# Token stage of a two-layer decoder step: bias loads on GpSimd's queue, weights queued ahead of later tokens, five token buffers, and the second weight group five tiles behind with its weights split in four parts

## The chip, the cores and the metric

One Trainium2 chip, one core of it. The metric is the device time of one execution in microseconds; lower is better. TensorE (PE) multiplies, ScalarE (ACT) and VectorE (DVE) prepare its operands and take its results, GpSimd (POOL) and SyncE (SP) mostly issue transfers; ACT can issue transfers too, from the same queue that holds its arithmetic.

## The reference, cut to what matters

The program is one inference step of a two-layer decoder for a prompt of 1024 tokens with 16 meta tokens ahead of it and for 8 sample sequences of 8 tokens: 1104 rows of 1024 values. The change touches only the first projection of the first layer, and there the value columns of `w_in` (1024 columns from column 1024 on) and its 16 gate columns:

```
def rmsnorm(x, g):
    r = lax.rsqrt(jnp.mean(xf * xf, axis=-1, keepdims=True) + EPS)
    return xf * r * g
...
p = rmsnorm(x, norm_a) @ w_in
v  = p[..., 2 * HK:2 * HK + HV]
gi = p[..., 2 * HK + 2 * HV:2 * HK + 2 * HV + H_A]
gf = p[..., 2 * HK + 2 * HV + H_A:]
li = softcap(gi + b_ig)
lf = log_sigmoid(softcap(gf + b_fg))
```

Everything is float32. The kernel gets that precision by splitting each operand into a high and a low part and adding three products.

## The kernel before, in words

The token stage is the function `values_a`. Its rows lie in nine tiles: tile 0 holds the 64 sample rows and the 16 meta rows, tiles 1 to 8 hold 128 prompt rows each. The value columns are made in four groups `c` of 256. The text calls group 0 the first group and group 3 the second group, since they are the two that run while the tokens come in; the second group also carries the 16 gate columns, so its products have 272 columns. Groups 1 and 2 follow after the loop. The weights of one group are two pieces `z` of 512 KB (rows 0 to 511 and rows 512 to 1023).

The steps, with the names that the text uses:

- `load(i)` (line 718) brings token tile i from memory into a buffer `xin`; four buffers exist. SP issues it, and it waits until the buffer's last reader is done.
- `fetch(c, z)` (line 650) brings a weight piece into one of two buffers `wraw`.
- T(i), in the code `turn(i)` (line 726): eight TensorE transposes of tile i into four PSUM buffers `xps`, two for a tile.
- `halves(i)` (line 734): ACT casts the transposed tile to the high part `xh`, DVE subtracts to get the low part `xl`, two instructions each.
- `halve(c, z)` (line 655): four times ACT scales 128 weight rows by the norm's gain into `whi`, and DVE makes `wlo`. For the second group a last pair of instructions does the same for the gate columns of the whole piece, columns 256 to 272 of `whi` and `wlo`.
- `keep(i)` (line 740): DVE copies the transposed tile into one of three buffers `hs`, and POOL issues the store of it (`hD`), for a later reload.
- `squares(i)` (line 747): ACT squares tile i with a running sum and takes the root; DVE later takes the reciprocal (line 783), the row's norm factor.
- V(c, i), in the code `values(c, i)` (line 671): 24 products for group c and tile i, and `out`, the ACT copy (line 681) that scales the result by the norm factor.

In this stage the order on PE, SP, DVE and ACT is the order in which the code is written; each engine takes its instructions strictly in that order. POOL's order, and the place of other functions' instructions between them (the biases of `rec_prep`, the page table of `cache_loads`), comes from the scheduler. Iteration i of the loop at line 769 does V(0, i), then T(i + 2) and `halves(i + 2)`, then the reciprocal and the copy out of V(0, i), then loads, `keep(i + 2)`, `squares(i + 2)`, perhaps a piece of the second group's weights, and last V(3, i - LAG) with LAG = 3. Both pieces of the second group are split in iterations 1 and 2, one whole piece in each.

Of the kernel before, what the change touches and what calls it, by code (L numbers as in the profile page):

```python
# [8 lines left out]
F32 = mybir.dt.float32  # L9
F32R = mybir.dt.float32r  # L10
I32 = mybir.dt.int32
AF = mybir.ActivationFunctionType
# [5 lines left out]
P = 128  # L18
D = 1024
# [9 lines left out]
NT = len(TT)  # L29
# [22 lines left out]
class PairWeights:  # L52
# [15 lines left out]
    def load(self, x):  # L68
        c0 = x % 2 * DFF + x // 2 * 2 * P
        for i, r in enumerate(self.plain(x)):  # L70
            self.net.nc.sync.dma_start(r, self.w[:, c0 + i * P : c0 + i * P + P].rearrange("(k p) n -> p k n", p=P))
# [560 lines left out]
def values_a(self, v, kp, gates, w_in, c3):  # L632

    nc, I = self.nc, self.I
    E = mybir.EngineType
# [4 lines left out]
    W, raws, xin, xps, hr = {}, {}, {}, {}, {}  # L640

    with ExitStack() as cw, self.pool("ppA0", bufs=4, space=PSUM) as pp:
        self.wpools(cw, 2, 4)
        wr = self.wp
        xr = cw.enter_context(self.pool("xr", bufs=3, side="right"))
        rr, ss = (xr.tile([P, NT], F32, name=nm, bufs=1) for nm in ("rr", "ss"))
# [3 lines left out]
        def fetch(c, z, queue=nc.sync):  # L650
            c0 = 2 * HA * DK + 256 * c
            raw = raws[c, z] = wr.tile([P, 4, 256], F32, name=self.uid("wraw"), tag="wraw", bufs=2)
            queue.dma_start(raw, w_in[4 * z * P : 4 * z * P + 4 * P, c0 : c0 + 256].rearrange("(k p) n -> p k n", p=P))

        def halve(c, z):
            raw = raws.pop((c, z))
            n = 272 if c == 3 else 256
            hi, lo = W[c, z] = [wr.tile([P, 4 * n], F32R, name=self.uid(nm), tag=nm, bufs=4).rearrange(
                "p (k n) -> p k n", k=4) for nm in ("whi", "wlo")]
            if c == 2:  # L660
                self.split(raw, hi, lo)
                return
            for k in range(4):
                y = hi[:, k, :256]
                nc.scalar.activation(y, raw[:, k], AF.Copy, scale=G(4 * z + k))
                nc.vector.scalar_tensor_tensor(out=lo[:, k, :256], in0=raw[:, k], scalar=G(4 * z + k),
                                               in1=y.bitcast(F32), op0=ALU.mult, op1=ALU.subtract)
            if c == 3:
                self.split(gw[:, 4 * z : 4 * z + 4], hi[:, :, 256:], lo[:, :, 256:])

        def values(c, i):
            n, m = 272 if c == 3 else 256, size(i)
            ps = pp.tile([P, 512], F32, name=self.uid("tmps"), tag="mm0")
            for k in range(KT):
                h, l = self.x_tile(i, k)
                wh, wl = W[c, k // 4]
                self.mm3(ps[:m, :n], h, l, wh[:, k % 4], wl[:, k % 4], k == 0, k == KT - 1)

            def out():
                r = 1.0 if c == 2 else rr[:m, i : i + 1]  # L680
                nc.scalar.activation(v(i)[:m, 2 * c : 2 * c + 2, :DV],
                                     ps[:m, :256].rearrange("p (h d) -> p h d", h=2), AF.Copy, scale=r)
                if c == 3:
                    nc.scalar.activation(gates[:m, i, :], ps[:m, 256:272], AF.Copy, scale=r)
            return out

        def reload(i):
            n, (t0, t1) = size(i), TT[i]
            y = hr[i] = xr.tile([P, KT, P], F32, name=f"hr{i}", tag="hr")
            nc.sync.dma_start(y[:, :, :n], self.hD[:, :, t0:t1])  # L690
# [21 lines left out]
        lx = ExitStack()  # L712
        lp = lx.enter_context(self.pool("lx"))
        tp = lx.enter_context(self.pool("lxp", bufs=4, space=PSUM))
        junk = lp.tile([P, D], F32, name="xsq")
        cell = lambda nm: lp.tile([P, D], F32, name=nm, tag="xin", bufs=4)

        def load(i):
            x = xin[i] = cell(f"xin{i}")
            if i == 0:  # L720
                nc.sync.dma_start(x[:NS], I["x_sample"].rearrange("b t d -> (b t) d"))
                nc.sync.dma_start(x[NS:T0], I["meta_tokens"])
            else:
                nc.sync.dma_start(x, I["x_prompt"][0, (i - 1) * P : i * P, :])

        def turn(i):
            n = size(i)
            for g in range(2):
                ps = xps[i, g] = tp.tile([P, 4, P], F32, name=self.uid("xps"), tag="xps")
                for k in range(4):  # L730
                    f = 4 * g + k
                    nc.tensor.transpose(ps[:, k, :n], xin[i][:n, f * P : (f + 1) * P], self.ident[:n, :n])

        def halves(i):
            n, (t0, t1) = size(i), TT[i]
            for g in range(2):
                ks = slice(4 * g, 4 * g + 4)
                self.split(xps[i, g][:, :, :n], xh[:, ks, t0:t1], xl[:, ks, t0:t1])

        def keep(i):  # L740
            n, (t0, t1) = size(i), TT[i]
            hs = lp.tile([P, KT, P], F32, name="hs", bufs=3)
            for g in range(2):
                nc.vector.tensor_copy(hs[:, 4 * g : 4 * g + 4, :n], xps.pop((i, g))[:, :, :n])
            nc.gpsimd.dma_start(self.hD[:, :, t0:t1], hs[:, :, :n])

        def squares(i):
            n = size(i)
            nc.scalar.activation(junk[:n], xin.pop(i)[:n], AF.Square, accum_out=ss[:n, i : i + 1])
            nc.scalar.activation(rr[:n, i : i + 1], ss[:n, i : i + 1], AF.Sqrt, scale=1.0 / D, bias=self.eps[:n])  # L750

        LAG = 3
        for z in range(2):
            fetch(0, z, nc.scalar)
            load(z)
        load(2)
        load(3)
        gw = xr.tile([P, P], F32, name="gw", tag="rb").rearrange("p (k n) -> p k n", k=KT)
        nc.scalar.dma_start(gw, w_in[:, 3072:3088].rearrange("(k p) n -> p k n", p=P))
        turn(0)  # L760
# [5 lines left out]
        halves(1)  # L766
        squares(0)
        keep(1)
        for i in range(NT + LAG):
            if i < NT:  # L770
                out = values(0, i)
            if i == 0:
                nc.vector.tensor_tensor(out=gw, in0=gw, in1=self.gain[:, G_A : G_A + KT].unsqueeze(2).broadcast_to([P, KT, 16]),
                                        op=ALU.mult)
                rows = xr.tile([P, P], F32, name="growsF", tag="rb")[: NG - G_F]
                self.gains(rows)
            if i + 2 < NT:
                turn(i + 2)
                halves(i + 2)
            if i == 0:  # L780
                squares(1)
            if i < NT:
                nc.vector.reciprocal(rr[: size(i), i : i + 1], rr[: size(i), i : i + 1])
                out()
            if i < 2:
                fetch(3, i)
            if i + 4 < NT:
                load(i + 4)
            if i + 2 < NT:
                keep(i + 2)  # L790
                squares(i + 2)
            if 1 <= i < 3:
                halve(3, i - 1)
            if i == 5:
                ps = tp.tile([P, 4, P], F32, name="gpsF", tag="xps").rearrange("p a b -> p (a b)")
                nc.tensor.transpose(ps[:, : NG - G_F], rows, self.ident[: NG - G_F, : NG - G_F])
                nc.vector.tensor_copy(self.gain[:, G_F:], ps[:, : NG - G_F])
                fetch(1, 0)
                fetch(1, 1)
                for x in range(3):  # L800
                    reload(x)
            if i == NT - 1:
                nc.gpsimd.dma_start(rD.rearrange("i p -> p i"), rr)
                for x in range(3):
                    spread(x)
            if 0 <= i - (NT + LAG - 3) < 2:
                halve(1, i - (NT + LAG - 3))
            if i >= LAG:
                values(3, i - LAG)()
        fetch(2, 0)  # L810
# [68 lines left out]
@_add(Net)  # L879
def phase_a(self, vt):  # L880
    nc, I, O = self.nc, self.I, self.O
    w_in = I["w_in_a"][0]
    qkD = self.dram.tile([8, P, T], F32, name="qkD")
    ogD = self.dram.tile([8, P, T], F32, name="ogD")
# [146 lines left out]
def rec_prep(self, kp, gates, rp, pp):  # L1031

    nc, I, O = self.nc, self.I, self.O
    tm, den, ssq = self.fin
    if True:

        bias = kp.tile([P, 16], F32, name="gbias")
        nc.scalar.dma_start(bias[:, :8], I["b_ig_a"][0].partition_broadcast(P))
        nc.scalar.dma_start(bias[:, 8:], I["b_fg_a"][0].partition_broadcast(P))
        m0 = kp.tile([HA, NB], F32, name="m0")  # L1040
        nc.scalar.dma_start(m0, I["state_m"][0].rearrange("b h -> h b"))
        selP = kp.tile([HA, 4, P], F32, name="selP")
        nc.gpsimd.memset(selP, 0.0)
        for j in range(4):
# [36 lines left out]
        if True:  # L1081
# [6 lines left out]
            e, w, li, lf, b, m = (rp.tile([HA, T], F32, name=s) for s in ("eA", "wA", "li", "lf", "bA", "mA"))  # L1088
# [18 lines left out]
            for s in range(NB):  # L1107
                c = slice(s * NQ, (s + 1) * NQ)
# [1931 lines left out]
```

## Time and profile before

| | us |
|---|---|
| median of 3 runs | 2832.24 (2831.84 to 2833.01) |
| the profiled execution, whole | 2829.72 |
| its span in the trace | 2828.0 |
| TensorE busy in the span | 2761.9 |
| TensorE not busy in the first 10 us / from 10 to 50 us | 6.67 / 3.46 |

The profiled execution is 2.5 us below the median, so a difference that is worked out in the trace is added to the median. Times inside the trace count from the span's start. In a timeline, a row has the start, the length, the engine, the line and operation, the result and its inputs, the count, and in brackets how long the engine was idle before it and what ended that. Consecutive products overlap, so the step from one start to the next tells the pace and not the length of one row. In a table of stretches the columns are the stretch, its length, then for each engine the busy time with its number of instructions, then the granted TensorE clock (1.00 is full), the mean busy share of the 16 transfer engines and GB/s.

### The profile page before, as it was taken

What the parts mean: (1) busy time and instruction counts of PE and PEld (TensorE: products, weight loads), DVE (VectorE), ACT (ScalarE), POOL (GpSimd) and SP (SyncE); (2) the same over time, 40 slices, a digit from 0 to 9 for tenths busy, and PEclk for the clock granted to TensorE, in tenths of its full rate; (3) what the DMA queues carried; (4) which work ended last, traced back from release to release, by engine and by line L of the source; (5) the groups of instructions that cost most, each with busy time, mean ns of one, the idle gap of its engine ahead of it and who ended that gap; (6) DMA issues with size and microseconds to landing.
All of it is one profiled execution on the core that took longest, in us unless ns stands there. A gap on an engine that the chain in (4) does not pass through costs nothing. (4 is left out here: it accounts for less than half of the span.)

```text
span 2828.0 us, 60538 instructions
## 1 busy us (share of the span) xinstructions
PE 2761.9 (98%) x23543; PEld 2650.3 (94%) x23543; DVE 1800.4 (64%) x4025; ACT 1177.3 (42%) x2299; POOL 836.0 (30%) x1313
## 2 busy tenths in 40 slices
PE   8999999999999999999999999999999999999998
PEld 8989889999999999999999888677999999999998
DVE  4632566888887765563455444777388888766556
ACT  5422453432322334443444445777343223323345
POOL 3122233132232332124453202544313223323111
PEclk9999999999999999999999999999999999999999
DMA  6666547245554375545444676442524555527556
GB/s 196 171 196 162 144 125 255 90 143 165 176 167 148 112 243 174 195 145 171 139 172 132 237 279 226 154 143 86 157 83 128 175 176 164 161 90 239 178 191 215
DMA packets 439001, 474.03 MB, mean 168 GB/s; under 512 B 41422, under 2 KB 365258, under 8 KB 437690
## 3 DMA queue, kind: packets, MB, share of 16 engines
q1 hardware_dynamic: 387522, 320.78, 36.8%
q0 software_dynamic: 43808, 143.17, 15.3%
q10 hardware_dynamic: 7384, 6.22, 0.7%
q8 instruction: 185, 3.03, 0.5%
q14 instruction: 102, 0.84, 0.1%
HBM read 322.84 MB, written 147.21 MB: 166 GB/s over the span
## 5 line engine op out<-in xcount | busy, mean ns | idle before, releaser
L1611 PE MATMUL m<-xh,slot 128*128 128x276 f32 x2752 | 541.3, 290 | 1.8 <-ACT fs L1640 1.8
L1611 PEld LDWEIGHTS m<-xh,slot 128*128 128x128 f32 x2752 | 440.4, 188 | 3.6 <-ACT fs L1640 2.2
L1611 PE MATMUL m<-xl,slot 128*128 128x276 f32 x1376 | 397.4, 289 | 0.0
L1611 PEld LDWEIGHTS m<-xl,slot 128*128 128x128 f32 x1376 | 259.1, 188 | 0.0
L193 PE MATMUL tmps<-slot,xh 128*128 128x256 f32 (+2 forms) x864 | 243.1, 281 | 0.0
L195 PE MATMUL tmps<-slot,xl 128*128 128x256 f32 (+2 forms) x864 | 240.6, 278 | 0.0
L194 PE MATMUL tmps<-slot,xh 128*128 128x256 f32 (+2 forms) x864 | 240.5, 278 | 0.0
L272 DVE TENSOR_TENSOR slot<-slot,slot 128x1024 fp32r<-128x1024 f32 x124 | 162.9, 1314 | 60.7 <-ACT slot L271 59.2
L271 ACT CAST slot<-slot 128x1024 fp32r<-128x1024 f32 x124 | 129.6, 1046 | 141.2 <-PE m L1611 111.7
L194 PEld LDWEIGHTS tmps<-slot,xh 128*128 128x128 f32 (+1 forms) x864 | 159.2, 184 | 0.1
L195 PEld LDWEIGHTS tmps<-slot,xl 128*128 128x128 f32 (+1 forms) x864 | 158.6, 184 | 0.0
L193 PEld LDWEIGHTS tmps<-slot,xh 128*128 128x128 f32 (+1 forms) x864 | 158.4, 183 | 0.2
L193 PE MATMUL mmA<-xh,whi 128*128 128x384 f32 (+1 forms) x384 | 135.1, 352 | 0.0
L194 PE MATMUL mmA<-xl,whi 128*128 128x384 f32 (+1 forms) x384 | 127.9, 333 | 0.0
L195 PE MATMUL mmA<-xh,wlo 128*128 128x384 f32 (+1 forms) x384 | 127.7, 333 | 0.0
L272 DVE TENSOR_TENSOR slot<-vA,slot 128x1024 fp32r<-128x1024 f32 (+1 forms) x59 | 82.2, 1396 | 32.6 <-ACT slot L271 31.5
L272 DVE TENSOR_TENSOR slot<-Ht,slot 128x1024 fp32r<-128x1024 f32 (+1 forms) x59 | 81.4, 1382 | 32.3 <-ACT slot L271 31.1
L271 ACT CAST slot<-Ht 128x1024 fp32r<-128x1024 f32 (+1 forms) x59 | 61.0, 1037 | 96.8 <-PE m L1611 92.9
L271 ACT CAST slot<-vA 128x1024 fp32r<-128x1024 f32 (+1 forms) x59 | 60.8, 1035 | 95.5 <-PE m L1611 90.5
L1715 DVE TENSOR_TENSOR ws<-ws 128x128 f32<-128x128 f32 x264 | 93.8, 355 | 8.9
L2862 ACT ACTIVATE s<-s,nb 128x272 f32<-128x272 f32 (+7 forms) x126 | 98.9, 786 | 0.0
L2897 ACT COPY th<-tp 128x768 f32<-128x768 f32 (+1 forms) x80 | 73.6, 920 | 53.7 <-PE tp L2889 30.5
(805 smaller groups left out, 8668.8 us busy)
## 6 DMA issues: line engine op xcount, KB each, us to landing
ws<-in_w_down SPq DMA_DIRECT2D x176, 128.0 KB, 2.8
sD<-ws SPq DMA_DIRECT2D x176, 128.0 KB, 2.3
slot<-sD SPq DMA_DIRECT2D x40, 512.0 KB, 4.2
slot<-in_w_gate_up SPq DMA_DIRECT2D x36, 512.0 KB, 3.9
kp<-in_cache_k SPq DMA_DIRECT2D x32, 512.0 KB, 6.7
vp<-in_cache_v SPq DMA_DIRECT2D x32, 512.0 KB, 5.1
vA<-in_w_gate_up SPq DMA_DIRECT2D x26, 512.0 KB, 4.4
Ht<-in_w_gate_up SPq DMA_DIRECT2D x26, 512.0 KB, 3.9
```

What stands on the lines that cost most here:

```text
L193: mm(ps, sh, mh, start=first, stop=False)
L194: mm(ps, sh, ml, start=False, stop=False)
L195: mm(ps, sl, mh, start=False, stop=last)
L271: self.nc.scalar.copy(hi, src)
L272: self.nc.vector.tensor_tensor(out=lo, in0=src, in1=hi.bitcast(F32), op=ALU.subtract)
L1611: nc.tensor.matmul(u.ps[h, b], w[p][:, k], x[q][:, k], start=first and k == i == 0, stop=k == 3 and i == 2, skip_group_check=True)
L1715: tt(out=o, in0=a, in1=b, op=ALU.subtract)
L2862: nc.scalar.activation(ss[z, u], ss[z, u], AF.Exp, bias=nb[:, z : z + 1], accum_out=sm[:, u, z : z + 1])
L2897: nc.scalar.copy(th.rearrange("p x z (u h q) -> p h (x z u) q", h=2, q=64)[:, :, :n], pt[:, :, :n])
```

## The change

- The two bias loads and the load of `state_m` go from ACT's queue to POOL's.
- The first piece of the first group's weights stays on ACT's queue; the second goes to SP's, behind token tile 0 and ahead of tiles 1 to 4.
- The buffer `xsq` that took the squares is gone (the squares overwrite the tile), and there are five token buffers. Five tiles are loaded ahead of the loop.
- The second group's pieces are fetched ahead of the loop and in iteration 0. Each piece is split in two steps of two weight blocks, one step in each of iterations 2, 3, 4 and 5; the gate columns of a piece are split with its second step.
- LAG is 5: V(3, 0) comes at the end of iteration 5.

```
-        def halve(c, z):
-            raw = raws.pop((c, z))
+        def halve(c, z, ks=range(4)):
+            raw = raws[c, z]
...
-            for k in range(4):
+            for k in ks:
...
-            if c == 3:
+            if c == 3 and ks[-1] == 3:
                 self.split(gw[:, 4 * z : 4 * z + 4], hi[:, :, 256:], lo[:, :, 256:])
...
-        junk = lp.tile([P, D], F32, name="xsq")
-        cell = lambda nm: lp.tile([P, D], F32, name=nm, tag="xin", bufs=4)
+        cell = lambda nm: lp.tile([P, D], F32, name=nm, tag="xin", bufs=5)
...
-            nc.scalar.activation(junk[:n], xin.pop(i)[:n], AF.Square, accum_out=ss[:n, i : i + 1])
+            x = xin.pop(i)[:n]
+            nc.scalar.activation(x, x, AF.Square, accum_out=ss[:n, i : i + 1])
...
-        LAG = 3
-        for z in range(2):
-            fetch(0, z, nc.scalar)
-            load(z)
-        load(2)
-        load(3)
+        LAG = 5
+        fetch(0, 0, nc.scalar)
+        load(0)
+        fetch(0, 1)
+        for x in range(1, 5):
+            load(x)
...
         squares(0)
         keep(1)
+        fetch(3, 0)
+        load(5)
         for i in range(NT + LAG):
...
             if i == 0:
                 squares(1)
+                fetch(3, 1)
+                load(6)
...
-            if i < 2:
-                fetch(3, i)
-            if i + 4 < NT:
-                load(i + 4)
             if i + 2 < NT:
                 keep(i + 2)
                 squares(i + 2)
-            if 1 <= i < 3:
-                halve(3, i - 1)
+            if i + 7 < NT:
+                load(i + 7)
+            if 2 <= i < 6:
+                halve(3, i // 2 - 1, range(2 * (i % 2), 2 * (i % 2) + 2))
...
-        nc.scalar.dma_start(bias[:, :8], I["b_ig_a"][0].partition_broadcast(P))
-        nc.scalar.dma_start(bias[:, 8:], I["b_fg_a"][0].partition_broadcast(P))
+        nc.gpsimd.dma_start(bias[:, :8], I["b_ig_a"][0].partition_broadcast(P))
+        nc.gpsimd.dma_start(bias[:, 8:], I["b_fg_a"][0].partition_broadcast(P))
...
-        nc.scalar.dma_start(m0, I["state_m"][0].rearrange("b h -> h b"))
+        nc.gpsimd.dma_start(m0, I["state_m"][0].rearrange("b h -> h b"))
```

How the instructions stand on the engines. First ACT at the program's start, before (`wraw_147` and `wraw_152` are the two pieces of the first group, `gw` the gate columns, `gbias` and `m` the loads of `rec_prep`, `xps_162` and `xps_167` the transposed tile 0):

```order
L653 DMA wraw_147<-in_w_in_a 128x4x256
L653 DMA wraw_152<-in_w_in_a 128x4x256
L759 DMA gw<-in_w_in_a 128x8x16
L1038 DMA gbias<-in_b_ig_a 128x8
L1039 DMA gbias<-in_b_fg_a 128x8
L1041 DMA m_1758<-in_state_m 8x8x1
L271 CAST xh<-xps_162 128x4x80
L271 CAST xh<-xps_167 128x4x80
L665 ACTIVATE whi_176<-wraw_147,gain 128x256 x4
L665 ACTIVATE whi_196<-wraw_152,gain 128x256 x4
```

The same place on ACT now (`xps_163` and `xps_168` are tile 0):

```order
L653 DMA wraw_146<-in_w_in_a 128x4x256
L759 DMA gw<-in_w_in_a 128x8x16
L271 CAST xh<-xps_163 128x4x80
L271 CAST xh<-xps_168 128x4x80
L665 ACTIVATE whi_177<-wraw_146,gain 128x256 x4
L665 ACTIVATE whi_197<-wraw_151,gain 128x256 x4
```

Four transfer issues have left the queue ahead of ACT's first cast. One of them stands on SP, whose start was this (tile 0 in two parts, tiles 1 to 3, the page table):

```order
L721 DMA xin_149<-in_x_sample 64x1024
L722 DMA xin_149<-in_meta_tokens 16x1024
L724 DMA xin_154<-in_x_prompt 128x1024
L724 DMA xin_156<-in_x_prompt 128x1024
L724 DMA xin_158<-in_x_prompt 128x1024
L1001 DMA ptab<-in_page_table 1x32
```

and is now this (`wraw_151` is the second piece of the first group, `wraw_221` the first piece of the second):

```order
L720 DMA xin_148<-in_x_sample 64x1024
L721 DMA xin_148<-in_meta_tokens 16x1024
L653 DMA wraw_151<-in_w_in_a 128x4x256
L723 DMA xin_153<-in_x_prompt 128x1024
L723 DMA xin_155<-in_x_prompt 128x1024
L723 DMA xin_157<-in_x_prompt 128x1024
L723 DMA xin_159<-in_x_prompt 128x1024
L1004 DMA ptab<-in_page_table 1x32
L653 DMA wraw_221<-in_w_in_a 128x4x256
```

Tile 1 (`xin_153`) now stands behind a weight piece on its queue, and a fifth tile ahead of the page table. The third place is ACT in iterations 1 and 2 before, where the second group's weights `whi_331` (piece 0) and `whi_392` (piece 1) are made between the copies out of V(0, 1), `tmps_280`, and V(0, 2), `tmps_343`:

```order
L681 ACTIVATE vA<-tmps_280,rr 128x2x128
L749 ACTIVATE xsq,ss<-xin_158 128x1024
L750 ACTIVATE rr<-ss,eps 128x1
L665 ACTIVATE whi_331<-wraw_270,gain 128x256 x4
L271 CAST whi_331<-gw 128x4x16
L271 CAST xh<-xps_368 128x4x128
L271 CAST xh<-xps_373 128x4x128
L681 ACTIVATE vA<-tmps_343,rr 128x2x128
L749 ACTIVATE xsq,ss<-xin_272 128x1024
L750 ACTIVATE rr<-ss,eps 128x1
L665 ACTIVATE whi_392<-wraw_321,gain 128x256 x4
L271 CAST whi_392<-gw 128x4x16
```

Now the last of these instructions stand in iterations 4 and 5, behind the copies out of V(0, 4), `tmps_442`, and V(0, 5), `tmps_495`; `whi_489` is piece 1 and `tmps_561` is V(3, 0):

```order
L681 ACTIVATE vA<-tmps_442,rr 128x2x128
L749 ACTIVATE xin_275,ss<-xin_275 128x1024
L750 ACTIVATE rr<-ss,eps 128x1
L665 ACTIVATE whi_489<-wraw_273,gain 128x256 x2
L271 CAST xh<-xps_520 128x4x128
L271 CAST xh<-xps_525 128x4x128
L681 ACTIVATE vA<-tmps_495,rr 128x2x128
L749 ACTIVATE xin_285,ss<-xin_285 128x1024
L750 ACTIVATE rr<-ss,eps 128x1
L665 ACTIVATE whi_489<-wraw_273,gain 128x256 x2
L271 CAST whi_489<-gw 128x4x16
L681 ACTIVATE vA<-tmps_561,rr 80x2x128
```

The cast of the gate columns of piece 1 is now the instruction directly ahead of the copy out of V(3, 0); before, two casts, a copy out of V(0, 3) and a tile's squares stood between the two. On PE, V(3, 0) stood behind V(0, 3) and T(5); it now stands behind V(0, 5) and T(7).

More of the change, by code (lines that the diff above doesn't have):

```diff
@@ L653, in fetch @@
             queue.dma_start(raw, w_in[4 * z * P : 4 * z * P + 4 * P, c0 : c0 + 256].rearrange("(k p) n -> p k n", p=P))
-        def halve(c, z):
-            raw = raws.pop((c, z))
+        def halve(c, z, ks=range(4)):
+            raw = raws[c, z]
             n = 272 if c == 3 else 256
-            hi, lo = W[c, z] = [wr.tile([P, 4 * n], F32R, name=self.uid(nm), tag=nm, bufs=4).rearrange(
+            hi, lo = W[c, z] = W.get((c, z)) or [wr.tile([P, 4 * n], F32R, name=self.uid(nm), tag=nm, bufs=4).rearrange(
                 "p (k n) -> p k n", k=4) for nm in ("whi", "wlo")]
@@ L881, in phase_a @@
     nc, I, O = self.nc, self.I, self.O
+    E = mybir.EngineType
     w_in = I["w_in_a"][0]
```

## The prediction

> **What bounds the kernel now.** I read the stretches of the stage first, then TensorE's timeline, then ACT's, since ACT ends the waits there.
>
> ```profile
> 0.00:10.00 10.00, 3.33 (x17) 2.83 (x17) 0.42 (x5) 2.01 (x4) 9.35 (x73) 1.00 0.81 250
> 10.00:20.00 10.00, 9.40 (x62) 8.93 (x62) 9.26 (x22) 8.61 (x21) 8.71 (x29) 1.00 0.61 155
> 20.00:30.00 10.00, 9.13 (x80) 8.97 (x79) 7.57 (x17) 8.05 (x18) 1.70 (x2) 1.00 1.03 378
> 30.00:40.00 10.00, 8.01 (x53) 7.44 (x52) 4.65 (x11) 6.48 (x18) 1.69 (x2) 0.83 0.88 262
> ...
> 40.00:120.00 80.00, 80.00 (x685) 79.78 (x685) 43.97 (x112) 35.66 (x71) 5.76 (x8) 1.00 0.54 149
> ```
>
> TensorE is idle for 10.1 us of the first 40, and busy without a break from 40 to 120 us. So the stage is bound by TensorE except at its start and at two places near 27 and 31 us. The timeline of TensorE names them:
>
> ```profile
> 5.81 1.30 PE L732 MATMUL xps<-ident,xin 80*128 80x80 f32 x8 [3.11 <-DMA xin<-in_meta_tokens]
> 8.21 1.97 PE L732 MATMUL xps<-ident,xin 128*128 128x128 f32 x8 [1.10 <-DMA xin<-in_x_prompt]
> 10.69 0.50 PE L193 MATMUL tmps<-whi,xh 128*80 128x256 f32 x1 [0.52 <-ACT whi L665]
> 15.85 1.03 PE L732 MATMUL xps<-ident,xin 128*128 128x128 f32 x8
> 19.46 1.04 PE L732 MATMUL xps<-ident,xin 128*128 128x128 f32 x8
> 23.17 1.03 PE L732 MATMUL xps<-ident,xin 128*128 128x128 f32 x8
> 27.80 1.06 PE L732 MATMUL xps<-ident,xin 128*128 128x128 f32 x8 [0.86 <-DMA xin<-in_x_prompt]
> 32.36 0.52 PE L193 MATMUL tmps<-whi,xh 128*80 128x272 f32 x1 [1.99 <-ACT whi L271]
> 35.46 0.41 PE L193 MATMUL tmps<-whi,xh 128*128 128x256 f32 x1
> 39.24 0.37 PE L193 MATMUL tmps<-whi,xh 128*128 128x272 f32 x1
> 42.34 0.28 PE L193 MATMUL tmps<-whi,xh 128*128 128x256 f32 x1
> 45.08 1.03 PE L732 MATMUL xps<-ident,xin 128*128 128x128 f32 x8
> 46.23 0.39 PE L193 MATMUL tmps<-whi,xh 128*128 128x272 f32 x1
> ```
>
> The transposes T(0) to T(5) start at 5.81, 8.21, 15.85, 19.46, 23.17 and 27.80; T(7) starts at 45.08. V(0, 0) starts at 10.69. T(5) waits 0.86 us for tile 5. At 32.36 V(3, 0) goes on with its second 12 products after 1.99 us; what released it is line 271, the cast of the gate columns, the last step of the second piece's split. V(3, 1) takes 42.34 - 39.24 = 3.10 us at full pace and V(0, 5) takes 45.08 - 42.34 = 2.74. The 12 products after the wait take 35.46 - 32.36 = 3.10 too, twice what 12 should, and the clock says why:
>
> ```profile
> 33.00:34.00 1.00, 1.00 (x5) 1.00 (x6) 1.00 (x2) 0.27 (x1) 0.00 (x0) 0.50 0.53 160
> 36.00:37.00 1.00, 1.00 (x11) 1.00 (x10) 0.00 (x0) 0.57 (x3) 0.62 (x1) 1.00 1.01 360
> ```
>
> The granted clock is 0.50 behind the wait and 1.00 some 3 us later. V(0, 0) runs at that pace as well: 10.69 to 15.85 is 5.16 us for the work of 2.74. Here the Trainium skill, "TensorE: Matmul & The Clock Gate", Part 1, says that the clock falls after an idle window of about 3.4 us and comes back after a busy one. By it the 1.99 us wait need not have cost the clock; the row decides that it did.
>
> **The change, part by part.**
>
> *Start: ACT's queue.*
>
> ```profile
> 3.13 5.43 ACTq L1038 DMA_DIRECT2D gbias<-in_b_ig_a  x1
> 8.60 0.45 ACTq L1039 DMA_DIRECT2D gbias<-in_b_fg_a  x1
> 9.09 0.35 ACTq L1041 DMA_DIRECT2D m<-in_state_m  x1
> 9.48 0.75 ACT L271 CAST xh<-xps 128x320 fp32r<-128x320 f32 x2 [6.53 <-PE xps L732]
> 12.61 1.70 ACT L665 ACTIVATE whi<-wraw,gain 128x256 fp32r<-128x256 f32 x4 [0.78 <-DMA wraw<-in_w_in_a]
> ```
>
> The three issues hold ACT until 9.44. T(0) ends at 7.11, so the first cast can come 2.4 us earlier. That is no gain by itself, because V(0, 0) stands behind T(1) on TensorE, and T(1) waits for tile 1, which landed at 8.2. The moved weights decide when that is now.
>
> ```profile
> 2.00:5.00 3.00, 0.24 (x1) 0.17 (x1) 0.17 (x1) 0.94 (x2) 3.00 (x14) 1.00 0.92 211
> 5.00:8.00 3.00, 1.30 (x8) 1.09 (x8) 0.00 (x0) 0.00 (x0) 3.00 (x32) 1.00 1.07 369
> 8.00:12.00 4.00, 3.19 (x12) 2.50 (x13) 2.06 (x6) 2.35 (x6) 4.00 (x20) 1.00 1.07 329
> 12.00:15.00 3.00, 3.00 (x16) 3.00 (x16) 2.26 (x7) 2.39 (x6) 3.00 (x11) 1.00 0.02 1
> ```
>
> The transfer engines are full from about 3 to 12 us (share 1.07). Now 328 KB of tile 0 (80 rows of 4 KB), two pieces of 524 KB and tile 1 of 524 KB, 1900 KB in all, move before tile 1 is complete, since the second piece is ahead of it on its queue and the first runs beside them. At the measured rates 633 KB are through at 5.0; the other 1267 KB at 369 GB/s take 3.4 us, to 8.4. The gate columns (66 KB) beside them add 0.2. The last piece before landed at 12.61, at most 1 us after the engines went quiet (the row from 12 on moves 1 GB/s), so I add 1: tile 1 lands at 9.7, 1.5 us later. The Trainium skill, "DMA: Bandwidth & Descriptors", "Issuing engines are not separate DMA queues", says the same: transfers from all issuers share the same 16 engines, so another queue saves issue time only. The share of 1.07 agrees.
>
> T(1) then takes its 1.97 us, and V(0, 0) starts at 11.8, 1.1 us later than 10.69; the weights are split by then. If all of V(0, 0) is at half pace as before, T(2) is 1.1 late. If half pace lasts only 3.1 us, as behind 32.36, counted from T(1)'s start, 1.1 us of V(0, 0) are slow (5 products) and 19 products take 2.74 x 19/24 = 2.2: V(0, 0) ends at 15.1, 0.75 early. I take 0.5 late, nearer to the row of V(0, 0) itself. Call this d.
>
> *Token loop: second group.* ACT's pace sets this part.
>
> ```profile
> 19.52 0.47 ACT L681 ACTIVATE vA<-tmps,rr 80x256 f32<-80x256 f32 x1 [0.55 <-DVE rr L783]
> 21.26 1.05 ACT L271 CAST xh<-xps 128x512 fp32r<-128x512 f32 x2
> 25.00 1.70 ACT L665 ACTIVATE whi<-wraw,gain 128x256 fp32r<-128x256 f32 x4
> 26.60 0.23 ACT L271 CAST whi<-gw 128x64 fp32r<-128x64 f32 x1
> 26.73 1.06 ACT L271 CAST xh<-xps 128x512 fp32r<-128x512 f32 x2
> 28.74 0.48 ACT L681 ACTIVATE vA<-tmps,rr 128x256 f32<-128x256 f32 x1 [0.94 <-DVE rr L783]
> 32.08 0.23 ACT L271 CAST whi<-gw 128x64 fp32r<-128x64 f32 x1
> ```
>
> From the cast of tile 3 at 21.26 to the split at 25.00 is 3.74 us: the cast, 0.94 us of waiting for DVE's reciprocal (which stands behind the low parts of the same tile), the copy out and the squares. A whole piece adds 26.60 - 25.00 = 1.60 and the gate cast 0.13 to the next start. TensorE's iteration, T to T, is 23.17 - 19.46 = 3.71. So ACT has no room in an iteration; whatever part of the weights it makes there puts it behind.
>
> Now: the cast of tile 3 can come 0.55 earlier, since DVE has done its copies of tiles 0 and 1 sooner and that wait goes: 20.71 + d. Tile 4 follows after 3.74, tile 5 after 3.74 + 0.80, tile 6 after 3.74 + 0.93, tile 7 after 3.74 + 0.80. The last step, behind tile 7's squares, ends with the gate cast of piece 1, which begins another 3.74 + 0.80 later: 20.71 + 5 x 3.74 + 4 x 0.80 + 0.13 = 42.74 + d. Before, TensorE started 0.28 after that cast (32.08 to 32.36), so 43.0 + d.
>
> TensorE is there sooner. Tile 5 is loaded ahead, so the 0.86 goes; with 3.71 an iteration T(7) starts at 23.17 + 3 x 3.71 = 34.3. From T(7) to V(3, ·) is 46.23 - 45.08 = 1.15, half of V(3, 0) is 1.55: 37.0 + d. The wait for the gate cast is then 6.0 us where it was 1.99. Splitting in four doesn't help: the 13th product reads the gate columns too, and they are made with the last quarter, in the iteration of V(3, 0) itself. Before, a whole iteration lay between.
>
> Behind the wait I take the 12 products at 3.10, as before: 46.1 + d, with V(0, 0) to V(0, 5), T(7) and V(3, 0) done. The kernel before has all this and V(3, 1) at 46.23, so without V(3, 1) it is at 43.13. The change is 3.0 + d behind. If half pace lasts a second such stretch, 1.55 more.
>
> *Edits at nothing.* Biases on POOL: three issues more.
>
> ```profile
> 3.27 0.52 POOL L227 DMA_DIRECT2D growsF<-in_norm_b  x1
> ```
>
> At 0.52 each they put the store of tile 0 behind them back by 1.6 us; the first to want its buffer again is DVE's copy of tile 3, and DVE has 2.4 us free in 20 to 30. If that cover is gone, a copy is 1.6 us late behind ACT's back, which is itself waited for. The biases are added only after the loop. Squares over the tile itself are the same instruction, and the fifth buffer lets a load start earlier, at nothing once tiles are there in time. SP waits longer for the page table, behind five tiles: the opening batch grows by 524 KB, 1.4 us at 369 GB/s, to about 14; tile 5's issue stands behind that, and the tile is wanted only at 23.17 + 3.71 = 26.9. Five tail products V(3, 4) to V(3, 8) replace three, with the same total; the later splits keep their distance from the end.
>
> *Sum* against the profiled 2829.72: 3.0 + 0.5 = 3.5, so 2833.2. The median of the runs is 2.5 above the profiled execution: 2832.24 + 3.5 = 2835.7. About 0.2%, 5.7 us, is what a measurement of this kernel can tell from no change; the forecast lies within it, on the slow side. Its own ends are 3.0 - 0.75 = 2.2 and 3.0 + 1.1 + 1.55 = 5.7: 2834.4 to 2837.9.
>
> **The rivals.**
>
> Slower by more: tile 1 is starved. The second piece and the gate columns' small rows share the engines with it, and it lands with the last of the opening batch, at 12.61. V(0, 0) would start at 14.7, d = 4.0, the sum is 7.0: 2839.2. It decides from a landing at 11.2 on. For it: the engines are full, 1.07. Against: tile 1 is third on its queue, and two tiles follow it. Chance 0.13.
>
> Faster: ACT keeps up. If the five waits of 0.94 went, the gate cast would come at 38.0 and TensorE wait 1.3 us, about as at T(5), behind which T(5) took 1.06 like its neighbours: no half pace. That gives back 4.7 + 1.55 = 6.2: 2832.24 - 2.7 = 2829.5. It decides where the cast comes before 38.5. Against: DVE still has the reciprocal behind the low parts. Chance 0.08.
>
> The change doesn't do what it says: ACT's earlier start and the later weights cancel, and the wait in V(3, 0) costs what the two old waits cost: 2832.2. Against: 6.0 is over twice 0.86 + 1.99. Chance 0.10.
>
> **How the numbers follow.** Forecast 0.69, rivals 0.13, 0.08 and 0.10. The range takes in the forecast's ends, the slow rival and no change: 2831.9 to 2839.7, leaving out the fast rival and tails. Slower by over 0.2%: the slow rival and 0.05 of the forecast's upper end, 0.18. Faster by over 0.2%: 0.02, since even the fast rival stays within. The rest, 0.80, is no change that can be told.
>
> **What would show it.** In the profile of the changed kernel: ACT's first cast near 7.1 and no bias on its queue; T(1) behind a wait for tile 1 until 9.7 (the slow rival: over 11.2); no wait at T(5); one wait of about 6 us ended by line 271 ahead of the 13th product of V(3, 0), with a granted clock of 0.50 behind it. I am wrong if that wait is under 3 us, if ACT's iteration with half a piece is not 4.5 us, or if waits outside the first 50 us move by more than 1 us.

## The result, and the profile after

| | before | after |
|---|---|---|
| median, 12 runs each on one chip | 2829.34 us (2825.62 to 2835.78) | 2833.99 us (2829.99 to 2838.24) |
| ratio, 95% interval | | 1.0016 [1.0009, 1.0023] |
| profiled execution | 2829.72 us | 2838.24 us |

The change costs 4.65 us in the medians, 0.16%. The predicted time was 2835.7 us, 3.5 above before; the sign, the size and the place came out, though not every term behind them. (The 3.5 stood on a median of 2832.24 in three runs; on that of the twelve it would have been 2832.8.) Executions scatter over 8 to 10 us and the profiled one after is the slowest of its twelve, so the whole time is too coarse a measure for what follows. One execution of before, beside the runs of the experiments, was slow (2996.55 us at a mean clock of 0.85) and is left out of every median and ratio below. I use a point inside the trace instead: the load of ACT's table for the gates' tanh, which starts as soon as the gates of V(3, 8), the last product of the stage, are copied out. It is called the stage end below. The view of that one line gives it, first before, then after:

```profile
L1083 ACT ACT_TABLE_LOAD  x1: 1283/1283/1283, 77.4 to 77.4; - x1
```

```profile
L1086 ACT ACT_TABLE_LOAD  x1: 1283/1283/1283, 83.4 to 83.4; - x1
```

6.0 us later. The rest of the difference between the two profiled executions (8.3 in the spans) comes later in the program. It is of the size of the scatter: in the twelve traces of this document the span less the stage end goes from 2746.3 to 2756.3 us. The stretches of after, with the columns as in the prediction:

```profile
0.00:10.00 10.00, 1.54 (x9) 1.26 (x9) 3.22 (x11) 4.75 (x11) 9.35 (x65) 1.00 0.84 235
10.00:20.00 10.00, 9.95 (x73) 9.96 (x74) 7.38 (x16) 7.20 (x16) 9.79 (x38) 1.00 0.89 291
20.00:30.00 10.00, 10.00 (x90) 9.82 (x88) 5.20 (x10) 5.86 (x14) 2.80 (x6) 1.00 0.94 310
30.00:40.00 10.00, 7.19 (x56) 6.22 (x54) 7.44 (x17) 8.05 (x20) 2.53 (x3) 1.00 0.46 137
40.00:50.00 10.00, 5.39 (x23) 5.09 (x24) 4.06 (x11) 4.21 (x11) 0.85 (x1) 0.71 0.89 242
50.00:60.00 10.00, 10.00 (x82) 10.00 (x81) 2.78 (x7) 3.88 (x9) 1.87 (x2) 0.95 0.70 158
```

TensorE now has no gap from 10 to 30, where it had 1.5 us; it loses 2.8 us from 30 to 40 and 4.6 from 40 to 50, and there the clock falls to 0.71. Its timeline:

```profile
5.83 1.30 PE L731 MATMUL xps<-ident,xin 80*128 80x80 f32 x8 [3.19 <-DMA xin<-in_meta_tokens]
10.05 1.97 PE L731 MATMUL xps<-ident,xin 128*128 128x128 f32 x8 [2.92 <-DMA xin<-in_x_prompt]
15.40 1.03 PE L731 MATMUL xps<-ident,xin 128*128 128x128 f32 x8
...
26.32 1.19 PE L731 MATMUL xps<-ident,xin 128*128 128x128 f32 x8
...
34.55 1.04 PE L731 MATMUL xps<-ident,xin 128*128 128x128 f32 x8
37.91 0.23 PE L798 MATMUL gpsF<-ident,growsF 48*128 48x48 f32 x1 [2.32 <-issue]
44.60 0.52 PE L193 MATMUL tmps<-whi,xh 128*80 128x272 f32 x1 [4.80 <-ACT whi L271]
```

T(0), T(1), T(2), T(5) and T(7) can be compared with the rows of before: T(1) waits for tile 1 until 10.05, T(5) has no wait. Then TensorE waits twice, 2.32 + 4.80 = 7.1 us. The second wait ends at 44.60 with the 13th product of V(3, 0), released by line 271. The first stands ahead of a small transpose for a later stage, `gpsF` (line 798), which the code puts into iteration 5 ahead of V(3, 0). The page names no releaser for it. The transpose takes one of the four buffers `xps`, and in the code the first to come free belongs to tile 6; DVE's copy of tile 6 is two instructions:

```profile
37.13 1.27 DVE L743 COPY hs<-xps 128x512 f32<-128x512 f32 x2
```

Half of it is over at about 37.8, and the transpose starts at 37.91. In LAG 7 and in the run with earlier steps, below, it also starts 0.1 us behind the middle of that copy (36.82 and 39.20). So this wait is for DVE, which follows ACT here, and not for the gate cast; V(3, 0) begins only behind it, at 38.06. It doesn't add to the end, since the gate cast comes later still. The clock behind the second wait:

```profile
45.00:46.00 1.00, 1.00 (x5) 0.88 (x5) 0.19 (x2) 0.00 (x0) 0.00 (x0) 0.50 1.01 287
...
50.00:51.00 1.00, 1.00 (x7) 1.00 (x6) 0.00 (x0) 0.00 (x0) 0.00 (x0) 0.50 1.24 217
51.00:52.00 1.00, 1.00 (x10) 1.00 (x10) 0.00 (x0) 0.00 (x0) 0.00 (x0) 0.98 1.21 286
```

0.50 from 44.60 to about 50.9, 6.3 us, twice the stretch of before. On ACT:

```profile
6.63 0.96 ACT L271 CAST xh<-xps 128x320 fp32r<-128x320 f32 x2 [3.68 <-PE xps L731]
...
20.11 1.06 ACT L271 CAST xh<-xps 128x512 fp32r<-128x512 f32 x2
22.11 0.48 ACT L681 ACTIVATE vA<-tmps,rr 128x256 f32<-128x256 f32 x1 [0.94 <-DVE rr L787]
23.85 1.05 ACT L271 CAST xh<-xps 128x512 fp32r<-128x512 f32 x2
28.04 0.48 ACT L681 ACTIVATE vA<-tmps,rr 128x256 f32<-128x256 f32 x1 [3.13 <-DVE rr L787]
...
30.58 1.05 ACT L271 CAST xh<-xps 128x512 fp32r<-128x512 f32 x2
...
35.25 1.05 ACT L271 CAST xh<-xps 128x512 fp32r<-128x512 f32 x2
...
39.79 1.05 ACT L271 CAST xh<-xps 128x512 fp32r<-128x512 f32 x2
...
44.32 0.23 ACT L271 CAST whi<-gw 128x64 fp32r<-128x64 f32 x1
```

The casts of tiles 3 to 7 start at 20.11, 23.85, 30.58, 35.25 and 39.79, the last gate cast at 44.32. One copy out, at 28.04, waited 3.13 us for the reciprocal and not 0.94 like its neighbours: 2.19 us that the sum did not have. DVE says why:

```profile
25.45 1.29 DVE L743 COPY hs<-xps 128x512 f32<-128x512 f32 x2 [3.38 <-DMA hD<-hs]
```

DVE's copy of tile 3, ahead of that reciprocal, waited 3.38 us for the store of tile 0 to leave its buffer.

### The profile page after: what moved, and what is told of

Read it like the earlier page. It is cut to its first block, busy times and chain, and to the rows that moved or that the text cites. A ratio compares the mean times of both kernels' runs of the same rounds, so it can differ in the third digit from the quotient of the medians.

```text
span 2836.3 us, 60540 instructions
## 1 busy us (share of the span) xinstructions
PE 2761.7 (97%) x23543; PEld 2651.1 (93%) x23543; DVE 1797.7 (63%) x4025; ACT 1176.0 (41%) x2299; POOL 837.0 (30%) x1316
```

## The experiments

Theory: TensorE waits because ACT makes the gate pieces of V(3, 0) late, and three things set how late: the steps' place (LAG 5, one half piece an iteration), the 0.94 us that ACT loses in each iteration to a reciprocal queued behind the low parts, and the late store of tile 0. Rivals: the start (small loads, order of weights, five buffers) costs the time; or the distance of five tiles costs it by itself, whatever ACT does. Each ratio is against before on the same chip; a table at the end of the section has all of them. The ratio is worked out from the single executions and need not be the quotient of the two medians.

**Two tiles more of distance.** In the changed kernel:

```
-        LAG = 5
+        LAG = 7
```

> Changed kernel with LAG 7: V(3, 0) comes two iterations later, everything else as changed. The stage's end is read at the table load for the gates' tanh: 77.4 us before, 83.4 changed. Theory (V(3, 0) stands too close behind the last step of the second group's weights): ACT's last gate cast stays near 44.3 us, no wait of V(3, 0) on it, no half clock behind it, stage end 77 to 78, so about 6 us less than changed and level with before. Rival 1 (the start and the transfers' order cost the time): stage end stays at 83. Rival 2 (the store wait of DVE on POOL's queue is all of it): the wait of 3.4 us on the store stays and so do 2 to 3 us of the loss: stage end 80 to 81.

```profile
L1086 ACT ACT_TABLE_LOAD  x1: 1283/1283/1283, 75.4 to 75.4; - x1
```

Without the wait in V(3, 0) the stage ends 8.0 us earlier than in after and 2.0 earlier than before, with everything else of the change in place; 77 to 78 was expected. The store was waited for 0.9 us here and not 3.4. Since the last gate cast still comes at 43.24, it is TensorE's arrival that counts: the cast may be late if nobody is there.

**The four steps one iteration earlier.**

```
-            if 2 <= i < 6:
-                halve(3, i // 2 - 1, range(2 * (i % 2), 2 * (i % 2) + 2))
+            if 1 <= i < 5:
+                halve(3, (i - 1) // 2, range(2 * ((i - 1) % 2), 2 * ((i - 1) % 2) + 2))
```

> Changed kernel with the four steps of the second group's weights in iterations 1 to 4 instead of 2 to 5; LAG stays 5. Theory: the last gate cast comes one ACT iteration earlier, near 40.6 us, the wait ahead of the 13th product of V(3, 0) shrinks to about 1 us, stage end 78 to 80 (83.4 changed). Rival (only the store wait of DVE, 3.4 us, makes ACT late): the wait stays over 3 us and the stage end over 82.

The last gate cast comes at 41.09, the wait at the 13th product is 0.27 us and the stage ends at 77.5, as before. TensorE loses less there, and in smaller pieces earlier (0.42, 0.29, 0.23 and 2.11 us), none of which cost the clock. The 2.11 are the wait of the small transpose. Both figures are better than expected (a wait of about 1 us, an end at 78 to 80), although DVE's wait for the store, 3.36 us, was there in full.

**The second group's schedule of before.** In the changed kernel:

```
-        LAG = 5
+        LAG = 3
-            if 2 <= i < 6:
-                halve(3, i // 2 - 1, range(2 * (i % 2), 2 * (i % 2) + 2))
+            if 1 <= i < 3:
+                halve(3, i - 1)
```

> Changed kernel with the second group's schedule of before (LAG 3, whole pieces in iterations 1 and 2); queues, load order and five token buffers as changed. It splits the 6.0 us that the stage lost in the profiles (end 77.4 before, 83.4 changed). Theory: the second group's place costs about 5, the rest of the change about 1 (no wait for tile 5, 0.86 less; T(2) within 0.5 us of before; DVE's copy of tile 3 waits for the store that POOL now issues later, up to 2 more on ACT's chain): stage end 77 to 79. Rival (load order and queues cost the time): stage end over 81.

The stage ends at 77.4, as before, and the ratio is 0.9997 [0.9987, 1.0007]. What is left of the change in this run (small loads on POOL, order of the weights, five buffers, squares in place) neither gains nor costs: the rival that puts the loss at the start is out. A loss like that of after appears only together with the new schedule of the second group. But DVE's wait for the store was 0.8 us here, so this run does not price a long one.

**The small loads alone, in the kernel before.**

```
-        nc.scalar.dma_start(bias[:, :8], I["b_ig_a"][0].partition_broadcast(P))
+        nc.gpsimd.dma_start(bias[:, :8], I["b_ig_a"][0].partition_broadcast(P))
```

and the other two alike.

> The kernel before with nothing but the two bias loads and the load of state_m on POOL's queue. Theory: ACT's first cast comes near 6.7 us, but V(0, 0) gains only its 0.5 us of waiting for the first weights, since it stands behind T(1) and T(1) behind tile 1; POOL's first store comes 1.5 us later and DVE's copy of tile 3 may wait for it: stage end 76.5 to 78.5 (77.4 before). Rival (ACT, held until 9.44 us, sets the start): everything comes 2 us or more earlier, stage end 75.4 or less.

ACT's first cast moves from 9.48 to 6.70, T(2) from 15.85 to 15.26; DVE now waits 1.1 us for the store of tile 0. The stage ends at 77.6 and the ratio is 1.0005 [0.9995, 1.0015]: freeing ACT's queue at the start buys nothing at the end.

**The small loads back on ACT, in the changed kernel** (the same three lines the other way).

> Changed kernel with the three small loads back on ACT's queue. Theory: the start hardly moves (V(0, 0) waits for T(1)); POOL's first store comes about 1.5 us earlier, DVE's wait for it falls from 3.4 to 1 to 2 us, and the last gate cast comes about 1.5 us earlier, so stage end 81 to 82.5 (83.4 changed). Rival (the loads on POOL are the whole loss): stage end 77 to 79. Other rival (they cost nothing there): 83 to 84.

```profile
2.56 0.70 ACTq L1041 DMA_DIRECT2D gbias<-in_b_ig_a  x1
3.28 0.99 ACTq L1042 DMA_DIRECT2D gbias<-in_b_fg_a  x1
...
43.39 0.23 ACT L271 CAST whi<-gw 128x64 fp32r<-128x64 f32 x1
```

The issues hold ACT for 2.0 us, not for the 6.2 of before, and its first cast still comes at 6.67: with the second weight piece off this queue the first of them takes 0.70 us where it took 5.43. By these rows moving the piece had freed ACT, and moving the small loads as well added nothing. DVE has no wait for a store (1 to 2 us were expected). From T(2) to the last gate cast are 26.73 us against 28.92 in after: 2.19 less, exactly the excess of the copy out at 28.04. But T(2) came at 16.66 in this execution, so the stage ends only 0.9 earlier, at 82.5. The wait at the 13th product is 4.79 us, with 6.8 us of half clock, and the ratio is 1.0015 where after has 1.0016: with this schedule the executions don't show that the store wait costs anything on the whole.

**The reciprocal ahead of the low parts.** The reciprocal of tile i stands ahead of `halves(i + 2)` instead of behind it. It needs only the squares of tile i, made two iterations earlier. First in the kernel before:

```
+            if i < NT:
+                nc.vector.reciprocal(rr[: size(i), i : i + 1], rr[: size(i), i : i + 1])
...
-                nc.vector.reciprocal(rr[: size(i), i : i + 1], rr[: size(i), i : i + 1])
```

> The kernel before with the same one move of the reciprocal and nothing of the change. Theory: ACT's iteration with a whole piece falls from 5.47 to 4.5 us, the last gate cast comes near 29.8 instead of 32.08, V(3, 0) doesn't wait (1.99 before) and the clock stays full: stage end 73.5 to 74.5, 3 to 4 us less than before, 0.12%. Rival (TensorE's waits there come from tile 5 being late, 0.86 us, which holds ACT too): the wait shrinks by less than 1 us and the stage end stays over 76.

```profile
L1084 ACT ACT_TABLE_LOAD  x1: 1283/1283/1283, 73.7 to 73.7; - x1
```

ACT's waits are gone, the last gate cast comes at 29.55, TensorE has no wait in V(3, 0), and the stage ends 3.7 us earlier: 2825.64 us, ratio 0.9985 [0.9976, 0.9994]. One line moved beats both kernels, by 0.15% against before.

The same line moved in the changed kernel:

> Changed kernel with one DVE instruction moved: the reciprocal of tile i stands ahead of the low parts of tile i + 2 instead of behind them. ACT then doesn't wait 0.94 us in each iteration, nor for the store that DVE waits for. Theory (ACT's iteration of 3.74 us without weights, 4.5 with half a piece, sets when the last gate cast comes): ACT's iteration falls to 2.8 and 3.6, the last gate cast comes near 38 to 39 us, the wait in V(3, 0) is under 2 us, stage end 76 to 77, about 3 us below before's whole. Rival 1 (the transfers' order costs the time): stage end over 82. Rival 2 (DVE's total work is the limit): ACT waits as long for other DVE instructions, last gate cast past 42.

```profile
25.42 1.29 DVE L743 COPY hs<-xps 128x512 f32<-128x512 f32 x2 [2.82 <-DMA hD<-hs]
```

The stage ends at 78.3, 1.3 us later than the upper end of what was expected, and the last gate cast comes at 40.33 (38 to 39 was expected). The store wait of DVE was there again and still reached ACT, and the wait at the 13th product was 2.78 us with 3.4 us of half clock some way behind it. With the schedule of before as well (LAG 3) the miss was larger:

> Candidate for the best: queues, load order and five buffers as changed, the second group's schedule of before, and the reciprocal ahead of the low parts. Theory: no wait for tile 5 and none in V(3, 0); DVE's copy of tile 3 may wait for its store without holding ACT: stage end 72.5 to 74 (73.7 with the move of the reciprocal alone), time within 0.05% of that kernel. Rival (the store wait of DVE still reaches TensorE through the transposes' buffers): a wait of 1 us or more ahead of T(5), stage end over 74.5.

```profile
25.23 1.29 DVE L743 COPY hs<-xps 128x512 f32<-128x512 f32 x2 [3.01 <-DMA hD<-hs]
```

```profile
28.34 0.48 ACT L681 ACTIVATE vA<-tmps,rr 128x256 f32<-128x256 f32 x1 [2.52 <-DVE rr L780]
31.68 0.23 ACT L271 CAST whi<-gw 128x64 fp32r<-128x64 f32 x1
31.96 0.51 PE L193 MATMUL tmps<-whi,xh 128*80 128x272 f32 x1 [2.06 <-ACT whi L271]
```

Stage end 78.1 where 72.5 to 74 were expected. The chain stands in four rows: the store, DVE's copy of tile 3, the reciprocal of the next iteration, which stands behind that copy, ACT's copy out, the gate cast, TensorE.

**Both repaired.** If the store is what ate the gain, the small loads have to go back to ACT along with the reciprocal's move. With LAG 3:

> The changed kernel with the second group's schedule of before, the reciprocal moved ahead of halves(i+2), and the three small loads back on ScalarE's queue; the five token buffers and the order of the weight loads stay. Theory (what the reciprocal's move lost in the run with the loads on GpSimd was the late store of tile 0, whose buffer VectorE wanted before it had landed): no wait of VectorE for a store, no wait of TensorE at the 13th product of V(3,0) over 0.3 us, last gate cast near 29.5, the token stage ends at 72.5 to 74 against 78.1 with the loads on GpSimd, and the time is 0.998 to 0.999 of before. Rival (the store's landing varies by itself and has nothing to do with the queue): a wait for the store of 2 to 3 us is there again, and the stage ends at 76 to 78, ratio 1.000.

```profile
29.59 0.23 ACT L271 CAST whi<-gw 128x64 fp32r<-128x64 f32 x1
29.87 0.35 PE L193 MATMUL tmps<-whi,xh 128*80 128x272 f32 x1 [0.28 <-ACT whi L271]
```

No store wait, gate cast at 29.59, stage end 73.6: 2824.30 us, ratio 0.9981 [0.9972, 0.9990], faster than both kernels. It isn't told from the one-line version (stage end 73.7, 0.9985): five buffers and the order of the weights add nothing to it that can be told. With LAG 5:

> The changed kernel with its second group five tiles behind, the reciprocal moved ahead of halves(i+2), and the three small loads back on ScalarE's queue. Theory (three terms add up: the store wait, ScalarE's wait for the reciprocal, and the gate pieces five tiles behind): without the first two the last gate cast is near 38, TensorE waits less than 1.5 us at the 13th product of V(3,0), the stage ends at 75 to 77 against 78.3 with the loads on GpSimd, ratio 0.999 to 1.000. Rival (the schedule five tiles behind alone costs the 5 to 6 us): the stage ends at 78 or later with a wait of 2 us or more at that product.

```profile
39.17 0.35 PE L193 MATMUL tmps<-whi,xh 128*80 128x272 f32 x1 [1.54 <-ACT whi L271]
```

The last gate cast comes at 38.89, the wait is 1.54 us (under 1.5 was expected) and costs no clock (1.00 from 30 to 50), the stage ends at 75.3. From T(2) to the gate cast are 22.40 us, 4.33 less than with the reciprocal where it was (26.73). So the three terms can be taken off one after another, and the schedule five tiles behind still ends 75.3 - 73.6 = 1.7 us after that of three. The medians of the two are 5.6 us apart, on one chip and with ratios whose intervals don't meet, more than the stage end accounts for. Behind the stage end this pair of traces differs by another 6.0 us. No run says whether that is scatter, so the second rival, that the distance costs time by itself, is cut down to 1.7 us by the stage end but not ruled out by the whole times.

All runs; the third column is the last gate cast less the start of T(2):

| kernel | DVE waits for a store, longest | T(2) to gate cast | stage end | median (before) | ratio [95%] |
|---|---|---|---|---|---|
| before | none | 16.23 | 77.4 | 2829.34 | |
| after | 3.4 | 28.92 | 83.4 | 2833.99 (2829.34) | 1.0016 [1.0009, 1.0023] |
| LAG 7 | 0.9 | 26.74 | 75.4 | 2827.45 (2829.50) | 0.9994 [0.9985, 1.0004] |
| steps earlier | 3.4 | 25.19 | 77.5 | 2829.79 (2829.50) | 1.0000 [0.9991, 1.0009] |
| schedule of before | 0.8 | 15.53 | 77.4 | 2827.93 (2831.23) | 0.9997 [0.9987, 1.0007] |
| before, small loads on POOL | 1.1 | 16.74 | 77.6 | 2831.32 (2831.23) | 1.0005 [0.9995, 1.0015] |
| small loads on ACT | none | 26.73 | 82.5 | 2835.34 (2831.23) | 1.0015 [1.0006, 1.0023] |
| before, reciprocal | 0.3 | 13.47 | 73.7 | 2825.64 (2829.50) | 0.9985 [0.9976, 0.9994] |
| reciprocal | 2.8 | 24.34 | 78.3 | 2829.06 (2829.50) | 1.0000 [0.9991, 1.0009] |
| LAG 3, reciprocal | 3.0 | 16.07 | 78.1 | 2829.02 (2831.23) | 0.9997 [0.9986, 1.0007] |
| LAG 3, reciprocal, loads on ACT | none | 13.46 | 73.6 | 2824.30 (2829.75) | 0.9981 [0.9972, 0.9990] |
| reciprocal, loads on ACT | 0.6 | 22.40 | 75.3 | 2829.86 (2829.75) | 1.0000 [0.9991, 1.0009] |

The stage end of the one profiled execution and the ratio go together within the intervals, in every row: 6.0 us of 2829 are 0.21% (measured 0.16), 3.8 are 0.13% (measured 0.19).

## Why the prediction was right

**The place and the mechanism held.** There was a long wait, ended by line 271, ahead of the 13th product of V(3, 0), with half clock behind it and no wait at T(5). It measured 4.80 us and not 6.0, mainly because the small transpose of iteration 5 kept V(3, 0) back by 2.32 us first; neither the prediction nor the order of the change has that transpose between T(7) and V(3, 0). The sum did not feel it, since the gate cast sets when TensorE goes on. One sign of being wrong did show: a wait behind the first 50 us moved by more than 1 us. At line 2606, which runs between 1619 and 1739 us, TensorE waits 1.3 us that it does not wait in before; at the other lines the waits moved by 1.0 us or less. None of the other changed kernels has more than 0.3 us at that line, so it is not tied to the change; its cause is not shown. Taking the wait away by distance alone (LAG 7) took the whole loss away.

**ACT's iteration held.** From the cast of tile 3 at 20.11 to that of tile 4 at 23.85 are 3.74 us; with half a piece and a gate cast the next took 35.25 - 30.58 = 4.67, with half a piece 39.79 - 35.25 = 4.54: the same figures as predicted. From T(2) to the last gate cast the prediction has 42.74 - 15.85 = 26.89; where no store was waited for, 26.73 and, with a wait of 0.9 us at another copy, 26.74 were measured.

**d was taken as +0.5 and came out as -0.45.** Tile 1 landed at 10.05 instead of 9.7; V(0, 0) began at 11.67 and ran at half pace only to 13.3, which is the working that the prediction gave less weight, 3.1 us counted from T(1)'s start. (From T(1)'s start to V(0, 0)'s are 1.62 us here and not the 1.97 of a whole T(1), since products overlap.) That sign can't be read from one execution: T(2) came at 15.40 here and at 16.50 with LAG 7, whose instructions up to T(2) are the same. In the nine traces with the new order of the weights it goes from 15.40 to 16.66, the middle one at 16.13, so d is nearer to +0.3 than to -0.45. The bounds, -0.75 and +1.1, hold all nine.

**"Edits at nothing" failed.** The biases on POOL were to be covered by 2.4 us that DVE has free between 20 and 30; they were not. That number is an engine's total over 10 us. The cover of this one copy stands in other rows of before, POOL's issue, the store's landing and DVE's copy of tile 3:

```profile
16.90 0.93 POOL L745 DMA_DIRECT2D hD<-hs  x1
...
hD<-hs POOLq DMA_DIRECT2D x1, 320.0 KB, 5.3
...
23.14 1.27 DVE L744 COPY hs<-xps 128x512 f32<-128x512 f32 x2
```

Landed at 16.90 + 5.3 = 22.2 and wanted at 23.14: 0.9 us free. After, from the same views:

```profile
18.35 0.91 POOL L744 DMA_DIRECT2D hD<-hs  x1 [0.21 <-issue]
...
hD<-hs POOLq DMA_DIRECT2D x1, 320.0 KB, 7.0
```

Issued 1.45 later (1.6 were foreseen), landed 1.7 later still, and wanted at 25.45 - 3.38 = 22.07, 1.07 earlier, since T(2) was 0.45 early and ACT's wait of 0.55 at the first copy out was gone. 1.45 + 1.7 + 1.07 - 0.94 = 3.3 us of wait against 3.38 in the row. "A copy is 1.6 us late behind ACT's back" was named as the price if the cover is gone; it was 2.19, and it was left out of the sum and of the range.

**"If half pace lasts a second such stretch"** was the unlikely end, and it is what happened: 6.3 us. V(3, 0)'s 12 products and V(0, 6) took 52.02 - 44.60 = 7.42 us for the work of 1.55 + 2.74, so 3.1 us were lost, 1.6 more than in the sum. With the small loads on ACT, the only other trace with so long a wait, it happened too.

**The sum.** TensorE restarted at 44.60 where 43.5 was predicted: -0.95 (d) + 2.19 (store) - 0.16 (the rest) = 1.1 later. With 1.6 for the clock, 3.5 + 1.1 + 1.6 = 6.2; the profiled execution has 6.0. The medians moved by 4.65, so this execution had it worse than most, and it is partly luck that 3.5 came as near: two terms were missing, and by the medians the typical execution has less of them than this trace. My estimate for the typical execution takes d at 0.3, the second stretch as in both traces and no store wait, since the ratio without one is the same: 3.0 + 0.3 + 1.6 = 4.9. By this estimate the second stretch is the term that was missing, and the store wait is a cost that comes and goes.

**The rivals.** Tile 1 landed at 10.05 and not 11.2 or later: the slower one fell. ACT did not keep up by itself: five of its copies out waited 0.94 us or more. But the faster rival's price was right as a mechanism: it had the gate cast at 38.0 with 1.3 us of wait and no half clock behind it; moving the reciprocal and the loads gave 38.89, 1.54 us and a clock of 1.00.

## What to carry to other kernels

Cover for a delayed store is the slack of the one instruction that wants its buffer, landing time against the time at which it is wanted, and not the idle share of its engine. When an in-order engine feeds the critical one, look for an operation in front of it that is ready long before and merely queued late: moving one reciprocal was worth more than the rearrangement of loads, buffers and weight steps. Splitting a preparation into parts spreads its load, but what the consumer waits for is the part it needs that is made last, here the gate columns.

## What the runs showed of the hardware

- The length of a wait alone does not tell what it costs in clock. In before 1.99 us were followed by half pace from the first product on. With the schedule of before in the changed kernel, 2.43 us were followed by a product at full pace and then by a slower one:

```profile
32.13 0.35 PE L193 MATMUL tmps<-whi,xh 128*80 128x272 f32 x1 [2.43 <-ACT whi L271]
32.65 0.52 PE L194 MATMUL tmps<-wlo,xh 128*80 128x272 f32 x1 [0.17 <-DVE wlo L272]
```

  Behind 2.78 and 3.34 us full clock lasted about 1.7 us more, then it fell; behind 1.54 it did not, nor behind 2.11 with the steps earlier. The low stretches had one of two lengths: a mean clock of 0.83 over 10 us (before, and three of the runs) is 3.4 us at 0.50; 0.66 over 10 us (two of the runs), or 0.71 and 0.95 over two times 10 us (after), are 6.8. The Trainium skill, "TensorE: Matmul & The Clock Gate", Part 1, says that the clock follows a window of 3.4 us that runs freely and isn't reset when a kernel starts, and that it falls after an idle window. One or two such lengths and the varying delay agree with it; its rule of an idle window doesn't fit waits of 1.99 and 2.06 us that cost the clock, and the measured rows decide. No run set the phase, so the cause stays open.

- POOL's 16 small selects at 7.5 us took 4.39 us where they had taken 2.34:

```profile
7.53 4.39 POOL L2471 TENSOR_SCALAR_AFFINE_SELECT rm<-rm 128x8 f32<-128x8 f32 x16
```

  In after DVE is busy for 4.36 of the 4.40 us from 7.50 to 11.90, in before for 1.96, all of it behind 9.94. The Trainium skill, "SBUF — State Buffer", "SBUF: two separate sides", says that a DVE operation with two inputs from that memory and a GpSimd operation that reads it share ports: the one that starts first keeps them for its whole instruction, and the other waits. DVE's splits of the weights, from 8.03 to 11.3 in after, have two such inputs. The rows agree; no run took it apart. It cost the store little: with the small loads on ACT the store was issued at 17.19, 0.3 us later than before, since POOL's later steps took less.

- The store of tile 0 took 4.2 to 7.4 us from issue to landing. With the small loads on ACT it was 5.1 to 5.5 in all five traces; on POOL it was 4.2, 5.4, 6.4, 6.7, 7.0, 7.0 and 7.4. Why it varies is not settled. A fourth buffer `hs`, which would take the wait away directly, wasn't tried.
